# Closing the output blocks earlier: the last two experts by token block, block 0 with its last gathered row

## The chip, the core and the metric

The kernel runs on one core of a Trainium2 chip. The core has five engines, each with an instruction stream of its own that is executed in order: TensorE (PE, matrix products; its weight loads are shown as PEld), VectorE (DVE), ScalarE (ACT, with activation tables), GpSimd (POOL) and SyncE (SP, which here only issues DMA transfers). Engines wait for one another with semaphores. The metric is the device time of one execution in microseconds (us), smaller is better. The kernel before takes 2018.77 us (median of 3 runs, 2015.53 to 2018.92).

## The reference

One layer of a decoder trunk on 512 tokens of width 1024: three gated token mixers, and then a PEER channel mixer, in which each token picks 8 x 16 single-neuron experts out of 16384, and a final normalisation. What the change touches is the end:

```
x = x + peer_ffn(rms_norm(x, g_ffn), w_peer_q, peer_sub_keys, peer_u, peer_v)
return rms_norm(x, g_final)

def peer_ffn(h, w_q, sub_keys, u, v):              # per block of 128 tokens xb
    ...                                            # ids, gate: the 8 x 16 best experts of each token
    act = gelu(einsum('nd,nhkd->nhk', xb, u[ids]))
    wgt = gate * act
    return einsum('nhk,nhkd->nd', wgt, v[ids])

def rms_norm(x, g):
    return x * rsqrt(mean(x * x, axis=-1) + 1e-6) * g
```

## The kernel before

The 512 tokens lie in four blocks of 128 (`NB = 4`); the residual stream is the tile `x1`, 128 partitions by 4 blocks by 1024. Everything up to the PEER mixer takes the first 784 us, retrieval of the experts and the building of gate matrices the next 248 us. Then two kinds of work run side by side.

*Block 0* (`GB = 1`) is computed sparsely, by `gathered` (L1318 to L1336): GpSimd fetches the 128 rows of `u` and then the 128 rows of `v` that each token chose, one row per token and transfer (`ug`); DVE forms a dot product of each row of `u` with the token (L1328), and adds each weighted row of `v` to `x1[:, 0]` (L1334).

*Blocks 1 to 3* (`ND = 3`, 384 tokens) are computed densely, by `experts` (L1352 to L1384): all 16384 experts, in 128 tiles of 128, each masked by the gate matrix. Per tile of experts: a load of 128 rows of `v` (`vload`, 512 KB, tile `wr`), split by ACT and DVE into a high and a low part (`wh` at L127, `wl` at L128); the hidden values `hg` times the gate tile `gj` (`gh`, L1370); a split of that product (`wgh` at L127, `wgl` at L128); and 18 products of 512 columns on TensorE (L1383): three (high by high, low by high, high by low) for each of two halves of the width and three token blocks. They accumulate over all 128 tiles in six PSUM banks `acc_o`, named `S`, `S`, `tr`, `tr`, `o`, `o`: two halves each for blocks 1, 2 and 3. The loop runs one tile ahead: in step n it prepares tile n + 1 and then issues the products of tile n. The buffers `wr`, `wh`, `wl`, `gh`, `wgh` and `wgl` are double, so the `wh` of a tile waits until the products of two tiles before have been issued through.

In the text an "expert" is one such tile of 128. The hidden values of the first 32 (`LEAD`) are computed early, while the gate matrices are built, and written to DRAM (`hd`); these 32 come last in the loop's order, and in their steps TensorE has only the 18 products, and SyncE issues three kinds of load: `wr` (512 KB), `hg` (192 KB) and, every eighth step, `gj` (1536 KB).

The order of all instructions on all engines is that of the program, which is written by hand. `weave` takes turns between the two generators: `experts` with the weight 750 and `gathered` with 258, so `gathered` ends some 30 experts before the end. Pools of tiles (`sbuf`) are stacked; a pool opened where another was closed takes its place, and its first writer waits for the last reader of what lay there.

After both generators have ended, the tail closes the blocks in the order 0, 1, 2, 3 (L1437 to L1449): it loads the gain row `gl` as a broadcast to 128 partitions; adds the two accumulators of a block to `x1` (L1445; block 0 has none); squares the block on ACT with an accumulated sum (`rms_stats`, L166), takes the square root of the scaled sum (L168, with a table load ahead of the first one), the reciprocal on DVE (L170), multiplies block, reciprocal and gain on DVE (L1448) and writes 512 KB out (L1449).

Of the kernel before, what the change touches and what calls it, by code (L numbers as in the profile page):

```python
# [10 lines left out]
F32 = mybir.dt.float32  # L11
# [4 lines left out]
AF = mybir.ActivationFunctionType  # L16
OP = mybir.AluOpType
# [5 lines left out]
NB = 4  # L23
D = 1024
KD = 8
M = 256
EPS = 1e-6
# [9 lines left out]
def weave(*streams):  # L37

    live = [[0.0, w, iter(gen)] for gen, w in streams]
    while live:  # L40
        item = min(live, key=lambda x: x[0])
        try:
            c = next(item[2])
            item[0] += (c if c else 1.0) / item[1]
        except StopIteration:
            live.remove(item)


def drain(gen):
    for _ in gen:  # L50
        pass
# [53 lines left out]
def layer(ctx: ExitStack, tc: tile.TileContext, A: dict, out: bass.AP, dbg=None):  # L105
    nc = tc.nc
    v, s, g, pe = nc.vector, nc.scalar, nc.gpsimd, nc.tensor
# [6 lines left out]
    def sbuf(stack, name, side="left"):  # L114
        return stack.enter_context(tc.tile_pool(name=name, bufs=1, side=side, reuse_waits="tile"))

    def psum(tag, shape, bufs=2, dt=F32):
        return ps.tile(shape, dt, tag=tag, name=tag, bufs=bufs)
# [7 lines left out]
    def split(hi, lo, src, eng=None):  # L126
        s.activation(hi, src, AF.Copy)  # L127
        (eng or v).tensor_tensor(lo, src, f(hi), op=OP.subtract)  # L128
# [3 lines left out]
    def wload(src, nk, n, pool=None, eng=None):  # L132

        pool = pool or wpool
        raw = pool.tile([128, nk * n], F32, tag="wr", name="wr", bufs=2)
        nc.sync.dma_start(raw, src)
        hi = pool.tile([128, nk, n], F32R, tag="wh", name="wh", bufs=2)
        lo = pool.tile([128, nk, n], F32R, tag="wl", name="wl", bufs=2)
        split(hi, lo, raw.rearrange("p (k n) -> p k n", n=n), eng or g)
        return hi, lo  # L140
# [19 lines left out]
    def bcast_row(dst, src):  # L160
        nc.sync.dma_start(dst, bass.AP(tensor=src.tensor, offset=src.offset, ap=[[0, 128], [1, D]]))

    def rms_stats(pool, rows):
        sq = pool.tile([128, D], F32, tag="sq", name="sq")
        ss = pool.tile([128, 1], F32, tag="ss", name="ss", bufs=2)
        s.activation(sq, rows, AF.Square, accum_out=ss)  # L166
        rt = pool.tile([128, 1], F32, tag="rt", name="rt", bufs=2)
        s.activation(rt, ss, AF.Sqrt, bias=eps, scale=1.0 / D)  # L168
        rs = pool.tile([128, 1], F32, tag="rs", name="rs", bufs=2)
        v.reciprocal(rs, rt)  # L170
        return rs
# [15 lines left out]
    GB = 1  # L187
    ND = NB - GB
# [178 lines left out]
    V = [ap_.tile([128, NB, 4, 2, 64], F32R, name=f"V{br}") for br in range(2)]  # L367
# [189 lines left out]
    for c in cross_order:  # L557
        n = int(c[1]) if c[1:].isdigit() else None
# [18 lines left out]
        elif len(c) == 3:  # L577
            br, b = int(c[1]), int(c[2])
# [393 lines left out]
    for at in attention():  # L972
# [5 lines left out]
        while done < goal:  # L978
            c = next(filler, None)
# [27 lines left out]
    x1 = xp.tile([128, NB, D], F32, name="x1")  # L1007
# [95 lines left out]
    hst = ExitStack()  # L1103
# [29 lines left out]
    def q_scores(hp, qT):  # L1133
        sp = psum("o", [128, NB, 128])
        for b in range(NB):
            pe.matmul(sp[:, b], qT[:, b * 128:(b + 1) * 128], skt[:, hp], start=b == 0, stop=b == 3,
                      skip_group_check=True)
        ss = qp_.tile([128, NB, 128], F32, name="ssb", bufs=2)
        s.activation(ss, sp, AF.Copy)
        return ss  # L1140
# [38 lines left out]
    for hp in range(16):  # L1179
# [3 lines left out]
        ss = q_scores(hp, qT)  # L1183
# [72 lines left out]
    def hidden(w):  # L1256
        p = psum("z", [128, T])
        mm3(p[:, 0:NT], w, (hfh, hfl), KD, xs=lambda x, k: x[:, k, t0:T])
        hg = ep.tile([128, NT], F32, name="hg", bufs=4)
        s.activation(hg, p[:, 0:NT], AF.Gelu)  # L1260
        return hg
# [49 lines left out]
    def gather(src, b, k):  # L1311
        row = ex_[0].tile([128, D], F32, tag="ug", name="ug", bufs=8)
        g.indirect_dma_start(out=row, out_offset=None, in_=src,  # L1313
                             in_offset=bass.IndirectOffsetOnAxis(ap=ids[:, b, k:k + 1], axis=0))
        return row

    def gathered(b):
        act = ex_[0].tile([128, 128], F32, name="act")  # L1318
        wgt = ex_[0].tile([128, 128], F32, name="wgt")
        todo = [(A["u_rows"], k) for k in range(128)] + [(A["v_rows"], k) for k in range(128)]  # L1320
        rows = {}
        for n in range(256 + AHEAD):
            if n < 256:
                rows[n] = gather(todo[n][0], b, todo[n][1])
            m = n - AHEAD
            if 0 <= m < 128:
                jk = ex_[0].tile([128, D], F32, name="jk")
                v.scalar_tensor_tensor(jk, rows.pop(m), 1.0, hf[:, b], op0=OP.mult, op1=OP.mult,  # L1328
                                       accum_out=act[:, m:m + 1])
            if m == 127:  # L1330
                s.activation(wgt, act, AF.Gelu)
                v.tensor_tensor(wgt, wgt, gate[:, b], op=OP.mult)
            if m >= 128:
                v.scalar_tensor_tensor(x1[:, b], rows.pop(m), wgt[:, m - 128:m - 127], x1[:, b],  # L1334
                                       op0=OP.mult, op1=OP.add)
            yield 1  # L1336

    acc_o = []

    order = list(range(LEAD, 128)) + list(range(LEAD))  # L1340
    U, G, V, H = {}, {}, {}, {}

    def gload(q_):
        G[q_] = wv2.tile([128, NT // 16, 8, 16], F32, name="gj", bufs=2)
        nc.sync.dma_start(G[q_].rearrange("p g c t -> p g (c t)"), gd[order[8 * q_] // 8])

    def vload(m):
        j = order[m]
        V[m] = wload(A["v_rows"][j * 128:(j + 1) * 128], 2, 512, wv2, v)

    def experts():
        acc_o.extend(psum(("S", "S", "tr", "tr", "o", "o")[i], [128, 512]) for i in range(2 * ND))  # L1352
        for n in range(-1, 128):
            m = n + 1
            if m < 128:
                j = order[m]
                if j >= LEAD:
                    U[m] = feed.take(("u", j))
                if m:
                    vload(m)  # L1360
                if m % 8 == 4 and m + 4 < 128:
                    gload(m // 8 + 1)
                if j < LEAD:
                    H[m] = ep.tile([128, NT], F32, tag="hg", name="hg2", bufs=4)
                    nc.sync.dma_start(H[m], hd[j])
                yield 3.9
                if j >= LEAD:
                    H[m] = hidden(U.pop(m))
                gh = ep.tile([128, NT], F32, name="gh", bufs=2)
                v.tensor_tensor(gh.rearrange("p (g t) -> p g t", t=16), G[m // 8][:, :, m % 8],  # L1370
                                H.pop(m).rearrange("p (g t) -> p g t", t=16), op=OP.mult)
                wh = ep.tile([128, NT], F32R, name="wgh", bufs=2)
                wl = ep.tile([128, NT], F32R, name="wgl", bufs=2)
                split(wh, wl, gh)
                V[m] = (wh, wl, V[m])
                if j >= LEAD:
                    yield 3.9
            if n >= 0:
                wh, wl, vw = V.pop(n)
                for b in range(ND):  # L1380
                    for i, (a, c) in enumerate(((wh, vw[0]), (wl, vw[0]), (wh, vw[1]))):
                        for half in range(2):
                            pe.matmul(acc_o[2 * b + half], a[:, b * 128:(b + 1) * 128], c[:, half],  # L1383
                                      start=n == 0 and i == 0, stop=n == 127 and i == 2)  # L1384

    gst = ExitStack()
    gp = sbuf(gst, "gp", "right")
# [40 lines left out]
    rqs.close()  # L1428
    ex_.append(sbuf(hst, "ex", "right"))
    wv2 = sbuf(hst, "wv2", "right")  # L1430
    vload(0)
    gload(0)
    drain(ld)
    weave((experts(), 750), (gath, 258 * GB))
    hst.close()

    with ExitStack() as fst:  # L1437
        fin = sbuf(fst, "fin", "right")
        gl = fin.tile([128, D], F32, name="gl")
        bcast_row(gl, A["g_final"])  # L1440
        for b in range(NB):
            if b >= GB:
                for half in range(2):
                    xs = x1[:, b, half * 512:(half + 1) * 512]
                    v.tensor_tensor(xs, xs, acc_o[2 * (b - GB) + half], op=OP.add)  # L1445
            rs = rms_stats(fin, x1[:, b])
            ob = fin.tile([128, D], F32, name="ob", bufs=2)
            v.scalar_tensor_tensor(ob, x1[:, b], rs, gl, op0=OP.mult, op1=OP.mult)  # L1448
            nc.sync.dma_start(out[b * 128:(b + 1) * 128], ob)  # L1449


def _consts():
# [83 lines left out]
```

## Time and profile before

| | us |
|---|---|
| median of 3 runs | 2018.77 (2015.53 to 2018.92) |
| profiled execution | 2020.64 |
| its span, first to last instruction | 2018.9 |
| start of the span to the query stage | 784 |
| query stage, retrieval, gate matrices (784 to 1032) | 248 |
| TensorE at rest between the stages (1032.1 to 1054.7) | 22.6 |
| experts with hidden values computed, beside the gathered block (1054.7 to 1866) | 811 |
| experts with stored hidden values (1866 to 2003.6) | 138 |
| after the last product (2003.6 to 2018.9) | 15.3 |

Over the whole span TensorE is busy 94%, DVE 66%, ACT 42%, GpSimd 34% of the time. The last gathered row is added at 1874.8 to 1876.0. A row of the timeline has the start, the duration, engine, line, operation, the tile written and those read, the shape, and in brackets the idle time of the engine just before it and who ended it. SPq is SyncE's queue; its rows are the issue of a transfer and not the transfer itself. Busy times of DMA are a mean over the core's 16 DMA engines. A span of several matrix products (x2, x8) runs from the start of the first to the end of the last; products overlap by a part of their length.

### The profile page before, as it was taken

To read this page: it belongs to the slowest core of one execution; us is meant where nothing else is said; L and a number is where in the kernel's file an instruction comes from. 1 tells how busy PE (TensorE), PEld (TensorE's weight loads), DVE (VectorE), ACT (ScalarE), POOL (GpSimd) and SP (SyncE) were. 2 spreads that over 40 slices of the span, in tenths; PEclk is the share of its full clock that TensorE was granted. 3 is DMA by queue.
4 is the path that set the end of the run, shared out by engine and by line. 5 is a ranking of instruction groups with operands and counts; after the bars stand their busy time and mean duration, and the time that the engine had idled before them with its cause. 6 is when DMAs were issued, how large, how long until landed. Compare 5 with 4: busy or idle time off the path is not lost.

```text
span 2018.9 us, 27913 instructions
## 1 busy us (share of the span) xinstructions
PE 1904.6 (94%) x10155; PEld 1661.6 (82%) x10155; DVE 1340.6 (66%) x2722; ACT 856.7 (42%) x1427; POOL 690.7 (34%) x551
## 2 busy tenths in 40 slices
PE   8999999999999996888849999999999999999996
PEld 7888888888888786887749999889888889988785
DVE  4353167765532699788737778777777877878555
ACT  6433266666522332657643333333333333333333
POOL 3223555555443231000013444444444444543000
PEclk9999999999999998999879999999999999999998
DMA  5315621212134221458797888898888888888663
GB/s 191 101 61 167 203 76 52 69 48 64 59 99 147 84 84 44 142 160 254 224 302 285 315 298 320 301 317 304 321 323 306 306 323 319 311 305 305 220 206 138
DMA packets 161918, 411.58 MB, mean 204 GB/s; under 512 B 13890, under 2 KB 72002, under 8 KB 159092
## 3 DMA queue, kind: packets, MB, share of 16 engines
q1 hardware_dynamic: 124916, 275.56, 40.1%
q0 software_dynamic: 36864, 134.23, 19.1%
q8 instruction: 80, 1.31, 0.3%
q14 instruction: 58, 0.48, 0.1%
HBM read 376.15 MB, written 38.84 MB: 206 GB/s over the span
## 4 chain that ended last, share of the span: by engine, by line
PE 54%; DVE 22%; DMA 12%; issue 6%; ACT 5%; SPq 0%; POOL 0%; ACTq 0%; DVEq 0%
PE z L148 28%; DMA wr<-in_v_rows_dram 9%; PE S L1383 5%; PE tr L1383 5%; PE o L1383 5%; DVE wl L128 4%; DVE x L1334 3%; PE o L900 2%; PE S L857 2%; ACT wh L127 2%; DVE jk L1328 2%; PE tr L889 2%; DMA wr<-in_u_t_dram 1%; DVE ob L1288 1%; DVE eq L1285 1%
## 5 line engine op out<-in xcount | busy, mean ns | idle before, releaser
L127 ACT ACTIVATE wh<-wr 128x1024 fp32r<-128x1024 f32 (+2 forms) x364 | 373.3, 1028 | 383.2 <-DMA wr<-in_v_rows_dram 223.9
L128 DVE TENSOR_TENSOR wl<-wr,wh 128x1024 fp32r<-128x1024 f32 x260 | 314.7, 1222 | 244.5 <-ACT wh L127 234.0
L148 PE MATMUL z<-hfh,wh 128*128 128x384 f32 (+1 forms) x1144 | 398.6, 348 | 26.8 <-ACT wh L127 26.8
L148 PE MATMUL z<-hfl,wh 128*128 128x384 f32 (+1 forms) x1144 | 394.3, 345 | 0.0
L1313 POOL DMA_INDIRECT ug<-in_u_rows_dram,ids x128 | 178.6, 1395 | 503.8 <-ACT stg L1302 257.8
L128 POOL TENSOR_TENSOR wl<-wr,wh 128x1024 fp32r<-128x1024 f32 (+2 forms) x104 | 226.6, 2180 | 322.5 <-ACT wh L127 253.1
L1313 POOL DMA_INDIRECT ug<-in_v_rows_dram,ids x128 | 183.7, 1435 | 218.3 <-DVE x L1334 194.0
L148 PE MATMUL z<-hfh,wl 128*128 128x384 f32 (+1 forms) x1144 | 232.4, 345 | 25.8 <-DVE wl L128 25.8
L148 PEld LDWEIGHTS z<-hfh,wh 128*128 128x128 f32 x1144 | 219.4, 192 | 37.1 <-ACT wh L127 28.4
L148 PEld LDWEIGHTS z<-hfh,wl 128*128 128x128 f32 x1144 | 204.3, 190 | 32.9 <-DVE wl L128 28.1
L148 PEld LDWEIGHTS z<-hfl,wh 128*128 128x128 f32 x1144 | 219.2, 192 | 8.8
L127 ACT ACTIVATE wgh<-gh 128x384 fp32r<-128x384 f32 x128 | 67.2, 525 | 340.1 <-DVE gh L1370 336.4
L1334 DVE SCALAR_TENSOR_TENSOR x<-ug,wgt,x 128x1024 f32<-128x1024 f32 x128 | 163.9, 1280 | 1.2
L1328 DVE SCALAR_TENSOR_TENSOR jk<-ug,hf 128x1024 f32<-128x1024 f32 x128 | 156.1, 1220 | 1.1
L148 PE MATMUL z<-hnh,wh 128*128 128x512 f32 x384 | 152.2, 396 | 3.0 <-ACT wh L127 2.9
L148 PE MATMUL z<-hnl,wh 128*128 128x512 f32 x384 | 150.4, 392 | 0.0
L128 DVE TENSOR_TENSOR wgl<-gh,wgh 128x384 fp32r<-128x384 f32 x128 | 71.9, 561 | 78.3 <-ACT wgh L127 78.3
L878 POOL TENSOR_SCALAR pr<-pr,sm,gsig 128x128 f32<-128x128 f32 (+3 forms) x128 | 78.7, 619 | 88.1 <-DVE sm L936 55.8
L892 DVE TENSOR_TENSOR PB<-tr,PB 128x128 fp32r<-128x128 f32 (+3 forms) x128 | 62.5, 489 | 62.2 <-ACT PB L891 61.7
L148 PE MATMUL z<-hnh,wl 128*128 128x512 f32 x384 | 99.2, 393 | 0.0
L1260 ACT ACTIVATE hg<-z 128x384 f32<-128x384 f32 x128 | 61.4, 480 | 87.8 <-PE z L148 84.6
L148 PEld LDWEIGHTS z<-hnh,wh 128*128 128x128 f32 x384 | 72.1, 188 | 18.8 <-ACT wh L127 3.5
(346 smaller groups left out, 3554.6 us busy)
## 6 DMA issues: line engine op xcount, KB each, us to landing
wr<-in_u_t_dram SPq DMA_DIRECT2D x128, 512.0 KB
wr<-in_v_rows_dram SPq DMA_DIRECT2D x128, 512.0 KB
wr<-in_w_z_dram SPq DMA_DIRECT2D x48, 512.0 KB
gd<-stg SPq DMA_DIRECT2D x24, 1024.0 KB
gj<-gd SPq DMA_DIRECT2D x16, 1536.0 KB
wr<-in_w_peer_q_dram SPq DMA_DIRECT2D x16, 512.0 KB
hd<-hg SPq DMA_DIRECT2D x32, 192.0 KB
hg<-hd SPq DMA_DIRECT2D x32, 192.0 KB
```

The costliest lines, as they stand in the source:

```text
L127: s.activation(hi, src, AF.Copy)
L128: (eng or v).tensor_tensor(lo, src, f(hi), op=OP.subtract)
L148: pe.matmul(p, w[a][:, k], xs(x[b], k), start=k == 0 and a == 0 and b == 0, stop=k == nk - 1 and a == 1)
L857: pe.matmul(sp[:, 0:nn], Q[gq, r][:, qb * 128:(qb + 1) * 128], KK[gq, br][i][:, 0:nn], start=i == 0, stop=i == 1)
L878: g.tensor_scalar(pr[:, 0:n], pr[:, 0:n], sm, gsig[:, qb, c:c + 1], op0=OP.mult, op1=OP.mult)
L889: pe.transpose(pt[:, kb], pr[:, kb * 128:(kb + 1) * 128], ident)
L892: return lambda: v.tensor_tensor(lo, pt[:, 0:qb + 1], f(hi), op=OP.subtract)
L1260: s.activation(hg, p[:, 0:NT], AF.Gelu)
L1313: g.indirect_dma_start(out=row, out_offset=None, in_=src, in_offset=bass.IndirectOffsetOnAxis(ap=ids[:, b, k:k + 1], axis=0))
L1328: v.scalar_tensor_tensor(jk, rows.pop(m), 1.0, hf[:, b], op0=OP.mult, op1=OP.mult, accum_out=act[:, m:m + 1])
L1334: v.scalar_tensor_tensor(x1[:, b], rows.pop(m), wgt[:, m - 128:m - 127], x1[:, b], op0=OP.mult, op1=OP.add)
L1383: pe.matmul(acc_o[2 * b + half], a[:, b * 128:(b + 1) * 128], c[:, half], start=n == 0 and i == 0, stop=n == 127 and i == 2)
```

## The change

Three things, in `gathered`, in `experts` and in what stood behind them.

- `closing(b)` is new. It does what the tail did for a block, but in two halves of 512 columns: addition of the accumulator (blocks 1 to 3), square with accumulated sum on ACT; the first half's sum is scaled by 1/1024 and given the epsilon on DVE, and it serves as the bias of the square root that has the second half's sum as input. `finish(b)` takes the root, the reciprocal and writes the block out as two halves of 256 KB. `closing` of one block calls `finish` of the one before it.
- In `experts` the step for expert 126 issues no products. The step for 127 issues those of 126 and 127 together, by token block: block 1's for both, `closing(1)`, block 2's for both, `closing(2)`, block 3's for both, `closing(3)`.
- `gathered` ends with `closing(0)` and `finish(0)`. The pool `fin` is opened, and `gl` is loaded, ahead of the first `vload`; `finish(3)` comes last.

In the order of instructions: on SyncE `gl` now stands between the last two writes of gate matrices (`gd`) and the first `wr` of `v`; block 0's two output transfers stand between the `hg` load of one expert and the `wr`, `gj` and `hg` loads of the next. On ACT block 0's two squares, a table load and the root stand between a `wh` and the next `wgh`; on DVE the scaling, the reciprocal and the two output multiplications stand between a `wl` and the next `gh`. GpSimd's order is the same. The number of products is the same; those of experts 126 and 127 have another order.

```diff
@@ gathered @@
                 v.scalar_tensor_tensor(x1[:, b], rows.pop(m), wgt[:, m - 128:m - 127], x1[:, b],
                                        op0=OP.mult, op1=OP.add)
             yield 1
+        closing(b)
+        finish(last.pop())
+
+    last, FS = [], {}
+
+    def finish(b):
+        rt = fin.tile([128, 1], F32, tag="rt", name="rt", bufs=4)
+        s.activation(rt, FS.pop((b, 1)), AF.Sqrt, bias=FS.pop((b, 0)), scale=1.0 / D)
+        rs = fin.tile([128, 1], F32, tag="rs", name="rs", bufs=4)
+        v.reciprocal(rs, rt)
+        for half in range(2):
+            c = slice(half * 512, half * 512 + 512)
+            ob = fin.tile([128, 512], F32, tag="fob", name="fob", bufs=4)
+            v.scalar_tensor_tensor(ob, x1[:, b, c], rs, gl[:, c], op0=OP.mult, op1=OP.mult)
+            nc.sync.dma_start(out[b * 128:(b + 1) * 128, c], ob)
+
+    def closing(b):
+        for half in range(2):
+            xs = x1[:, b, half * 512:half * 512 + 512]
+            if b >= GB:
+                v.tensor_tensor(xs, xs, acc_o[2 * (b - GB) + half], op=OP.add)
+            sq = fin.tile([128, 512], F32, tag="fsq", name="fsq")
+            ss = FS[b, half] = fin.tile([128, 1], F32, tag=f"fs{half}", name="fs", bufs=4)
+            s.activation(sq, xs, AF.Square, accum_out=ss)
+            if half == 0:
+                v.tensor_scalar(ss, ss, 1.0 / D, EPS, op0=OP.mult, op1=OP.add)
+        for d in last:
+            finish(d)
+        last[:] = [b]
@@ experts @@
-            if n >= 0:
-                wh, wl, vw = V.pop(n)
-                for b in range(ND):
+            if n < 0 or n == 126:
+                continue
+            for b in range(ND):
+                for k in ((126, 127) if n == 127 else (n,)):
+                    wh, wl, vw = V[k]
                     for i, (a, c) in enumerate(((wh, vw[0]), (wl, vw[0]), (wh, vw[1]))):
                         for half in range(2):
                             pe.matmul(acc_o[2 * b + half], a[:, b * 128:(b + 1) * 128], c[:, half],
-                                      start=n == 0 and i == 0, stop=n == 127 and i == 2)
+                                      start=k == 0 and i == 0, stop=k == 127 and i == 2)
+                if n == 127:
+                    closing(GB + b)
+            V.pop(n)
@@ the end of layer @@
     wv2 = sbuf(hst, "wv2", "right")
+    fin = sbuf(hst, "fin", "right")
+    gl = fin.tile([128, D], F32, name="gl")
+    bcast_row(gl, A["g_final"])
     vload(0)
     gload(0)
     drain(ld)
     weave((experts(), 750), (gath, 258 * GB))
+    for b in last:
+        finish(b)
     hst.close()
-
-    with ExitStack() as fst:
-        fin = sbuf(fst, "fin", "right")
-        gl = fin.tile([128, D], F32, name="gl")
-        bcast_row(gl, A["g_final"])
-        for b in range(NB):
-            if b >= GB:
-                for half in range(2):
-                    xs = x1[:, b, half * 512:(half + 1) * 512]
-                    v.tensor_tensor(xs, xs, acc_o[2 * (b - GB) + half], op=OP.add)
-            rs = rms_stats(fin, x1[:, b])
-            ob = fin.tile([128, D], F32, name="ob", bufs=2)
-            v.scalar_tensor_tensor(ob, x1[:, b], rs, gl, op0=OP.mult, op1=OP.mult)
-            nc.sync.dma_start(out[b * 128:(b + 1) * 128], ob)
```

## The prediction

> **What bounds it.** I read the page's slices first (TensorE close to full in nearly all of them), then busy time by stretch, then the timeline of the three places that the diff touches: the closing of block 0 near 1875 us, the last two experts, and everything after the last product.
>
> ```profile
> 1878.00:2003.60 125.60, 125.59 (x538) 100.55 (x537) 68.08 (x91) 47.62 (x62) 0.00 (x0) 1.00 0.58 199
> 2003.60:2018.90 15.30, 0.00 (x0) 0.00 (x0) 6.73 (x10) 4.33 (x9) 0.00 (x0) 0.64 0.32 127
> ```
>
> Columns: stretch, length, busy us (instructions) of PE, weight load, DVE, ACT, POOL, then granted clock, DMA share, GB/s. From 1878 on TensorE never rests: 125.6 / 538 = 0.233 us per 512-wide product, 18 x 0.233 = 4.2 us per expert. A TensorE stall put into this stretch is therefore paid in full. The 15.3 us after the last product have no TensorE work at all; only there can the change gain.
>
> **The tail it wants to shorten.** Before, block 3 ends so:
>
> ```profile
> 2010.75 1.28 DVE L1445 TENSOR_TENSOR x<-x,o 128x512 f32<-128x512 f32 x2
> 2012.07 1.06 ACT L166 ACTIVATE sq<-x 128x1024 f32<-128x1024 f32 x1 [2.75 <-DVE x L1445]
> 2013.03 0.19 ACT L166 ACTIVATION_READ_ACCUMULATOR sq<-x 128x1 f32 x1
> 2013.25 0.29 ACT L168 ACTIVATE rt<-ss,eps 128x1 f32<-128x1 f32 x1
> 2013.57 0.16 DVE L170 RECIPROCAL rs<-rt 128x1 f32<-128x1 f32 x1 [1.54 <-ACT rt L168]
> 2013.77 1.28 DVE L1448 SCALAR_TENSOR_TENSOR ob<-x,rs,gl 128x1024 f32<-128x1024 f32 x1
> ```
> ```profile
> 2015.50:2017.40 1.90, 0.00 (x0) 0.00 (x0) 0.00 (x0) 0.00 (x0) 0.00 (x0) 0.50 0.69 276
> ```
>
> Each block is a chain of 4.2 us and three of them follow one another, with block 0's in front. The last `ob` ends at 2015.05; issue, transfer (the second fence: 276 GB/s x 1.9 us, the 512 KB of the last output) and receipt take the other 3.85 us to 2018.9.
>
> **Part 1: products by block, blocks in halves (tail).** No product is added; what moves is that the S products of expert 127 come 6 instead of 18 products after those of 126 begin. Its operands do not come earlier, because ACT, DVE and the loads keep their order:
>
> ```profile
> 1994.80 1.06 ACT L127 ACTIVATE wh<-wr 128x1024 fp32r<-128x1024 f32 x1 [0.77 <-PE o L1383]
> 1997.70 0.53 ACT L127 ACTIVATE wgh<-gh 128x384 fp32r<-128x384 f32 x1 [1.84 <-DVE gh L1370]
> 1998.26 0.56 DVE L128 TENSOR_TENSOR wgl<-gh,wgh 128x384 fp32r<-128x384 f32 x1 [0.67 <-ACT wgh L127]
> ```
> ```profile
> 1995.03 0.63 PE L1383 MATMUL S<-wh,wgh 128*128 128x512 f32 x2
> ...
> 2002.96 0.63 PE L1383 MATMUL o<-wl,wgh 128*128 128x512 f32 x2
> ```
>
> `wh` of 127 waits for the buffer that 125's products release (1994.80), then `wl`, `gh`, `wgh` follow; `wgh` is done at 1998.23. Expert 126 starts at 1995.03; its six S products end at 1996.43. So TensorE waits 1.8 us for `wgh`, and about 0.2 more for `wgl` (1998.82) and restarts: products end 2.0 us later. In before's clock: S complete 2000.0, tr 2002.8, o 2005.6.
>
> The closings then run: per half an addition (1.28 / 2 = 0.64), a square of 512 with its accumulator read; the first half's sum is scaled by a small DVE instruction *before* DVE may add the second half.
>
> ```profile
> L1041 ACT ACTIVATE sq<-x 128x512 f32<-128x512 f32 x8 | 5.0, 630 | 11.1 <-DVE x L1038 9.3 <-ACT sq L1041 1.8
> 1999.29 1.28 ACT L168 ACT_TABLE_LOAD   x1
> ```
>
> With 0.63 + 0.19 less 0.09 overlap = 0.73 for a square: block 2's first addition starts at 2002.7 (when tr is done), square to 2004.1, scale to 2004.3, second half added to 2004.9, squared to 2005.65, root of block 1 to 2006.0, reciprocal to 2006.2, block 1's two outputs to 2007.45. Only now does DVE take block 3's first addition, though its products ended at 2005.6: DVE and ACT are the bound again. Block 3: added 2008.1, squared 2008.85, scaled 2009.0, added 2009.65, squared 2010.4; block 2's root, reciprocal and two outputs to 2012.2 stand ahead of block 3's reciprocal (2012.3); its outputs end at 2012.95 and 2013.6. That is 1.45 us before 2015.05. The last transfer is half as large: the 3.85 us become about 3.3 (an estimate from the 1.9 us of data: half of it, 0.95, would be saved if the other half were through by then; it is issued only 0.65 earlier, so about 0.55 is). Tail together: 2.0 us gained; bounds: 3.0 if the wait for `wgh` were free, 0.5 if the closings interlock worse. The table load (1.28 us) leaves the tail but lay beside TensorE's last products.
>
> **Part 2: block 0 closed with its last gathered row.** These instructions leave a place where they ran beside expert 127 and enter every queue near 1876 us:
>
> ```profile
> 1874.76 1.28 DVE L1334 SCALAR_TENSOR_TENSOR x<-ug,wgt,x 128x1024 f32<-128x1024 f32 x1
> 1875.96 0.55 DVE L1370 TENSOR_TENSOR gh<-gj,hg 128x384 f32<-128x384 f32 x1
> 1877.18 0.56 DVE L128 TENSOR_TENSOR wgl<-gh,wgh 128x384 fp32r<-128x384 f32 x1 [0.67 <-ACT wgh L127]
> 1878.13 1.23 DVE L128 TENSOR_TENSOR wl<-wr,wh 128x1024 fp32r<-128x1024 f32 x1 [0.39 <-ACT wh L127]
> 1879.28 0.55 DVE L1370 TENSOR_TENSOR gh<-gj,hg 128x384 f32<-128x384 f32 x1
> ```
> ```profile
> 1877.06 1.04 ACT L127 ACTIVATE wh<-wr 128x1024 fp32r<-128x1024 f32 x1
> 1879.94 0.53 ACT L127 ACTIVATE wgh<-gh 128x384 fp32r<-128x384 f32 x1 [1.84 <-DVE gh L1370]
> ```
> ```profile
> 1881.62 0.63 PE L1383 MATMUL S<-wh,wgh 128*128 128x512 f32 x2
> ...
> 1885.83 0.63 PE L1383 MATMUL S<-wh,wgh 128*128 128x512 f32 x2
> ```
>
> Call the experts whose products start at 1881.62 and 1885.83 B and C. The new order puts the closing between B's `wl` (1878.13) and B's `gh` (1879.28) on DVE, and between `wh` (1877.06) and `wgh` (1879.94) on ACT. ACT: two squares from 1878.1 to 1879.55, table load to 1880.9, root to 1881.2. DVE has the scale, then waits, reciprocal to 1881.4, two outputs to 1882.7; only then B's `gh`, 3.4 us late. B's `wgh` is ready at 1883.85, when TensorE wanted it at 1881.62: a stall of 2.3 us, 2.5 with the restart. Those who wait on this: B's products, and through them all later ones.
>
> The larger price is SyncE's queue:
>
> ```profile
> 1874.87 0.33 SPq L136 DMA_DIRECT2D wr<-in_v_rows_dram  x1
> 1875.25 0.42 SPq L1345 DMA_DIRECT2D gj<-gd  x1
> 1875.73 0.43 SPq L1365 DMA_DIRECT2D hg<-hd  x1
> 1879.39 0.33 SPq L136 DMA_DIRECT2D wr<-in_v_rows_dram  x1
> ```
> ```profile
> 1875.50:1882.00 6.50, 6.50 (x28) 4.86 (x27) 3.82 (x6) 2.59 (x4) 0.00 (x0) 1.00 0.94 355
> ```
>
> SyncE issues C's three loads at 1874.87 to 1875.73. In the changed order block 0's two output issues stand ahead of them, and they wait for the outputs at 1882.1 and 1882.7. So `wr` of C goes out at about 1883.15, 8.3 us late, `gj` at 1883.55, `hg` at 1884.0. Window row: 355 GB/s x 6.5 us = 2.3 MB, which is `wr`, `gj` and `hg` (0.52 + 1.57 + 0.20 MB); the small `hg` has landed only when that much is through, at 1882.0, 7.1 us after the issue of `wr`. Moved: 1883.15 + 7.1 = 1890.25. C's `gh` needs that `hg`: 1890.3; `wgh` 0.66 behind its start and 0.53 long: ready 1891.5; products of C at 1891.55 instead of 1885.83. Together with a slower restart this is 5.9 us, the 2.5 us of B contained in it. D's `wr`, issued at 1884.6 and next in the line, lands near 1892.1 (0.5 MB more): split, `gh`, `wgh` done by 1895.6, before C's products end at 1896.0; no more is lost. Bounds: 2.5 (the loads hidden after all) and 7.8 (the 512 KB written ahead of `wr` add their own 1.9 us). I take 5.9, since `wr`, `gj` and `hg` are the same transfers as in the row.
>
> **Clock.** B leaves a TensorE gap of 2.3 us, C one from the end of B's products (1883.9 + 4.4 = 1888.3) to 1891.55, above 3 us. Before shows what gaps do:
>
> ```profile
> 842.05 1.69 PE L148 MATMUL z<-hfh,wl 128*128 128x384 f32 x8 [2.34 <-DVE wl L128]
> 853.55 2.50 PE L148 MATMUL z<-hfh,wl 128*128 128x384 f32 x8 [1.91 <-DVE wl L128]
> 853.60:858.00 4.40, 4.40 (x17) 4.30 (x18) 4.30 (x8) 1.91 (x2) 0.00 (x0) 0.61 0.56 164
> ```
>
> After a gap of 2.34 us eight products took 1.69 us, after one of 1.91 us 2.50: the granted clock there was 0.61 over 4.4 us, that is 0.39 x 4.4 = 1.7 us of full clock lost. A gap above 3 us I expect to cost this once: 1.5 us (bounds 0 and 3, the tail's 1.8 us gap included). [...]
>
> **Part 3: `gl` and the new pool.** The 512 KB broadcast moves from 1989.65 to ahead of the first load of V.
>
> ```profile
> 1028.48 3.92 SPq L1304 DMA_DIRECT2D gd<-stg  x2
> 1048.88 0.35 SPq L136 DMA_DIRECT2D wr<-in_v_rows_dram  x1
> ...
> 1054.71 0.69 PE L148 MATMUL z<-hfh,wh 128*128 128x384 f32 x1 [22.62 <-ACT wh L127]
> 1048.50:1050.00 1.50, 0.00 (x0) 0.00 (x0) 0.00 (x0) 0.00 (x0) 0.00 (x0) 0.50 0.12 8
> ```
>
> TensorE stands still there until that load is split. `gl` is issued right behind the gate writes, at about 1032.5; its data follow theirs and fall mostly into the 1.5 us in which the queue moves 8 GB/s. Bounds 0 and 3 us; I take 0.5.
>
> **Sum.** -2.0 + 5.9 + 1.5 + 0.5 = +5.9 us. The profiled execution took 2020.64 (span 2018.9), 1.9 above the median; on the median 2018.77 that is 2024.7.
>
> **Rivals.**
> - *Covered closing* (not slower): ACT and DVE idle enough that block 0's closing hides and C's loads still arrive. It needs C's `hg` landed by 1883.6, so SyncE's issue by about 1876.5, but the outputs it waits for are made after 1881. Then only the tail counts: 2018.77 - 2.0 = 2016.8. Chance 0.08.
> - *Only DVE pays*: the late loads are quick, since nothing else is in the queue, and catch up with B's delay: -2.0 + 2.5 + 0.5 = +1.0, 2019.8. Against it: `gj` of 1.5 MB between `wr` and `hg`. Chance 0.18.
> - *No half clock*: 2023.2. For it the 2.34 us row, against it the 1.91 us row. Chance 0.17. [...]
> - *Heavier*: the tail's gap halves the clock too and `gl` delays the first load by 2 us or more: +1.5 +1.7 = 2027.9. Chance 0.15.
> - The forecast: 0.42, own range 2022.5 to 2027.
>
> **Chances.** 0.2% is 4 us, about what a measurement of this kernel can tell from no change: bounds 2014.7 and 2022.8. Faster takes half of the first rival and a little for what I do not see, 0.05; within takes the rest of the first, the second and the lower part of the third and of the forecast, 0.32; slower the remaining 0.63. The range 2018 to 2029 leaves out the first rival and the end of the heavier one.
>
> **What would show it.** In the profile after: DVE's `gh` of the expert behind block 0's outputs about 3.4 us late; the next `wr` issue behind the output issues; TensorE gaps of about 2.3 and 3.3 us near 1882 to 1892 and one of 1.8 us before the S products of 127, granted clock below 1 behind one; from the last product to the end 11 to 12 us instead of 15.3; no table load there. I am wrong if TensorE has no gap behind block 0's closing, or if the last products' end moves by less than 4 us.

## The result, and the profile after

The changed kernel takes 2024.55 us (median of 15 runs, 2017.72 to 2028.54), the kernel before 2018.92 us in the same comparison (15 runs, 2014.00 to 2022.40). The ratio is 1.0027, with a 95% interval of 1.0017 to 1.0036: slower by 3.4 to 7.3 us. The profiled execution took 2028.54 us (span 2026.8), 7.9 us more than that of before (span 2018.9). The steps below are accounted in these two executions; 2.3 us of their difference do not stand in the medians: the profiled execution is the slowest of its 15.

The closing of block 0 on DVE, from the timeline of the kernel after (start, duration, operation, tiles, shape, and the idle time before it with its ender):

```profile
1878.57 1.22 DVE L128 TENSOR_TENSOR wl<-wr,wh 128x1024 fp32r<-128x1024 f32 x1 [0.39 <-ACT wh L127]
...
1881.56 0.16 DVE L1347 RECIPROCAL rs<-rt 128x1 f32<-128x1 f32 x1 [1.70 <-ACT rt L1345]
1881.76 1.41 DVE L1351 SCALAR_TENSOR_TENSOR fob<-x,rs,gl 128x512 f32<-128x512 f32 x2
1883.09 0.55 DVE L1400 TENSOR_TENSOR gh<-gj,hg 128x384 f32<-128x384 f32 x1
...
1892.62 0.56 DVE L1400 TENSOR_TENSOR gh<-gj,hg 128x384 f32<-128x384 f32 x1 [1.88 <-DMA hg<-hd]
```

The same place on ACT, which DVE waited 1.70 us for, and in SyncE's queue of issues:

```profile
1879.94 1.28 ACT L1345 ACT_TABLE_LOAD   x1
...
1888.43 1.06 ACT L127 ACTIVATE wh<-wr 128x1024 fp32r<-128x1024 f32 x1 [4.18 <-DMA wr<-in_v_rows_dram]
```
```profile
1882.54 1.00 SPq L1352 DMA_DIRECT2D out_dram<-fob  x2
1883.63 0.39 SPq L136 DMA_DIRECT2D wr<-in_v_rows_dram  x1
1884.08 0.44 SPq L1375 DMA_DIRECT2D gj<-gd  x1
1884.57 0.42 SPq L1395 DMA_DIRECT2D hg<-hd  x1
1885.10 0.36 SPq L136 DMA_DIRECT2D wr<-in_v_rows_dram  x1
```

In the order of the prediction's letters: B's `gh` follows block 0's outputs at once, at 1883.09. C's three loads are issued only after both output issues, from 1883.63 on, and C's `gh` starts at 1892.62 with the landing of `hg`; the last issue shown is D's `wr`. The 1.5 MB of `gj` are not for C: the program loads them for the eight experts from number 104 on, and C is number 100, but C's `hg` stands behind them in the queue. What TensorE makes of it (same view, TensorE's rows; the first is the start behind the rest between the stages):

```profile
1054.73 0.69 PE L148 MATMUL z<-hfh,wh 128*128 128x384 f32 x1 [22.85 <-ACT wh L127]
...
1884.31 0.77 PE L1415 MATMUL S<-wh,wgh 128*128 128x512 f32 x2 [2.08 <-ACT wgh L127]
...
1893.85 0.73 PE L1415 MATMUL S<-wh,wgh 128*128 128x512 f32 x2 [3.44 <-ACT wgh L127]
...
1899.81 0.63 PE L1415 MATMUL S<-wh,wgh 128*128 128x512 f32 x2
...
2004.81 0.63 PE L1415 MATMUL S<-wh,wgh 128*128 128x512 f32 x2
...
2008.07 0.74 PE L1415 MATMUL S<-wh,wgh 128*128 128x512 f32 x2 [1.70 <-ACT wgh L127]
```

The others are the first S products of B, C, D (the expert after C), 126 and 127. Before, B started at 1881.62, C at 1885.83 and D at 1890.03. The rests of 2.08 and 3.44 us are new, and so is the 1.70 before the S products of 127. Busy time by stretch (columns as in the prediction: stretch, length, PE, PEld, DVE, ACT, POOL, granted clock, DMA share, GB/s):

```profile
1884.50:1892.60 8.10, 5.91 (x18) 4.20 (x17) 1.57 (x2) 1.06 (x1) 0.00 (x0) 0.79 1.01 358
1885.30:1892.60 7.30, 5.11 (x16) 3.69 (x15) 1.22 (x1) 1.06 (x1) 0.00 (x0) 0.80 0.99 372
1884.87:1888.28 3.41, 3.41 (x9) 2.71 (x9) 0.00 (x0) 0.00 (x0) 0.00 (x0) 0.50 0.98 302
1895.10:1898.50 3.40, 3.40 (x10) 2.62 (x9) 2.20 (x3) 0.52 (x1) 0.00 (x0) 0.50 0.44 119
2015.46:2026.80 11.34, 0.00 (x0) 0.00 (x0) 5.99 (x12) 2.11 (x9) 0.00 (x0) 0.61 0.38 139
```

While C's loads are under way the DMA engines are full (shares of 1.01 and 0.99, first two rows; the second begins where both of block 0's outputs have landed). Behind each of the two rests TensorE runs 3.4 us at half clock (granted clock 0.50, third and fourth row). After the last product 11.3 us are left instead of 15.3 (last row).

The 7.9 us, from these rows against those of before:

| step | us | how |
|---|---|---|
| ahead of the closing | +0.44 | the expert before B starts at 1877.64 and not 1877.20 |
| B late | +2.25 | 1884.31 - 1881.62 - 0.44 |
| C late, beyond B | +5.33 | 1893.85 - 1885.83 = 8.02, less 2.69 |
| C's products, half clock and restart | +1.76 | C to D takes 5.96 and not 4.20 |
| rest before 127's S products | +2.1 | last product ends 11.87 later, 9.78 of it from above |
| after the last product | -4.0 | 11.34 and not 15.30 |

### The profile page after: what moved, and what is told of

It is laid out like the page before. It is cut to its first block, busy times and chain, and to the rows that moved or that the text cites. A ratio compares the mean times of both kernels' runs of the same rounds, so it can differ in the third digit from the quotient of the medians.

```text
span 2026.8 us, 27937 instructions
## 1 busy us (share of the span) xinstructions
PE 1908.5 (94%) x10155; PEld 1662.9 (82%) x10155; DVE 1342.3 (66%) x2730; ACT 858.3 (42%) x1435; POOL 688.4 (34%) x551
## 4 chain that ended last, share of the span: by engine, by line
PE 62%; DVE 19%; DMA 9%; ACT 5%; issue 4%; SPq 0%; POOL 0%; ACTq 0%; DVEq 0%
PE z L148 32%; PE tr L1415 7%; PE S L1415 6%; PE o L1415 6%; DMA wr<-in_v_rows_dram 6%; DVE wl L128 3%; DVE x L1334 3%; PE o L900 2%; PE S L857 2%; ACT wh L127 2%; PE tr L889 2%; DMA wr<-in_u_t_dram 1%; DVE ob L1288 1%; DVE eq L1285 1%; DVE oa L1283 1%
## 5 line engine op out<-in xcount | busy, mean ns | idle before, releaser
L1415 PE MATMUL S<-wh,wgh 128*128 128x512 f32 x256 | 81.5, 400 | 12.0 <-ACT wgh L127 11.9
```

## The experiments

Single executions of one kernel scatter by 8 to 16 us from lowest to highest, those of before too, and most of that arises before the places that the change touches (the last product of hidden values starts between 1852 and 1861 us). So for each run the stretch from the start of that last product to the end of the span is given beside the ratio. It is read from TensorE's rows in the timeline of the profiled execution. Each ratio is to executions of the kernel before that were taken beside that run:

| kernel | to 126's first S product | from there to the end | sum | ratio to before, 95% interval |
|---|---|---|---|---|
| before | 137.66 | 23.84 | 161.5 | |
| after | 147.78 | 21.96 | 169.7 | 1.0027 (1.0017 to 1.0036) |
| block 0 late | 137.63 | 24.33 | 162.0 | 1.0002 (0.9986 to 1.0019) |
| block 0 early alone | 146.15 | 22.06 | 168.2 | 1.0044 (1.0029 to 1.0059) |
| old product order | 146.77 | 22.14 | 168.9 | 1.0051 (1.0036 to 1.0065) |
| outputs behind loads | 142.12 | 23.48 | 165.6 | 1.0017 (1.0003 to 1.0031) |
| outputs one step later | 141.85 | 21.95 | 163.8 | 1.0009 (0.9995 to 1.0022) |
| gaps filled | 145.47 | 21.96 | 167.4 | 1.0024 (1.0013 to 1.0036) |
| block 0 in pieces | 137.78 | 21.94 | 159.7 | 0.9993 (0.9979 to 1.0007) |
| pieces and plain tail | 137.00 | 17.56 | 154.6 | 0.9967 (0.9951 to 0.9983) |

The stretch scatters too. The change, "block 0 early alone" and "old product order" run the same instructions up to expert 126 and take 147.78, 146.15 and 146.77 us, so a difference of 1.6 us between single executions shows nothing there; the four kernels without a rest behind block 0 (before, block 0 late and the two in pieces) lie between 137.00 and 137.78.

The theory: the change loses in one place, behind block 0's closing, through DVE and ACT (B), SyncE's queue (C) and the clock; and it gains 2 us in the tail through halves and product order. Rivals: the product order or the early `gl` costs the time; the queue matters little and DVE alone pays; the clock plays no part; the tail's gain has another source.

**Each part alone.** Without the early closing of block 0, which goes ahead of block 1's in the last step:

```diff
@@ gathered @@
-        closing(b)
-        finish(last.pop())
@@ experts @@
+            if n == 127:
+                closing(0)
+                finish(last.pop())
             for b in range(ND):
```

> Products of 126 and 127 by block and closings in halves as in the change, but block 0 is closed in its old place, behind the last operand of expert 127. Theory (the loss lies in the closing of block 0 between the experts): no TensorE gap and no half clock near 1880 us, products end about 2 us later than before because of the wait for wgh of 127, and the tail is little shorter since block 0's outputs again stand ahead of DVE's first addition: 2019 to 2020 us against 2018.9 of before. Rival (the new order of the products is the loss): 2022 us or more.

The ratio is 1.0002 (0.9986 to 1.0019), and the way to expert 126 is that of before, 137.6 us. So the loss sits in block 0's early closing. The early `gl` and the new pool, which this kernel has too, show no cost: the rest between the stages, where they would be paid, lasts 22.73 us and 22.62 before (the ratio alone would leave room for 3.8 us). But the tail, with products by block and all halves, is not shorter: 24.3 us. DVE's rows:

```profile
2002.75 1.42 DVE L1349 SCALAR_TENSOR_TENSOR fob<-x,rs,gl 128x512 f32<-128x512 f32 x2
2004.08 0.68 DVE L1356 TENSOR_TENSOR x<-x,S 128x512 f32<-128x512 f32 x1
```

Block 1's first addition starts without idle time behind block 0's outputs, 7.75 us after 126's first S product at 1996.33. TensorE is slowed here from 2000.76 to 2004.17 (two products take 1.05 us and not 0.63, as behind C's rest in the change, where the granted clock is 0.50), behind its rest of 1.70 us ahead of 127's S products, but none of DVE's additions in this tail waits for a product, so that does not lengthen it. The other half, block 0 early with the old tail for blocks 1 to 3 (and two buffers for `fob` instead of four):

```diff
@@ experts @@
-            if n < 0 or n == 126:
+            if n < 0:
...
-                for k in ((126, 127) if n == 127 else (n,)):
+                for k in (n,):
...
-                if n == 127:
-                    closing(GB + b)
@@ the end of layer @@
-    for b in last:
-        finish(b)
+    fin2 = sbuf(hst, "fin2", "right")
+    for b in range(GB, NB):
...
+        rs = rms_stats(fin2, x1[:, b])
+        ob = fin2.tile([128, D], F32, name="ob", bufs=2)
```

> Only block 0 is closed early, with gl ahead of the first load of V; experts and the tail of blocks 1 to 3 are as before. Theory: both TensorE gaps (2.1 and 3.4 us) and one stretch at half clock that costs, 9 us together; the tail gains 1.7 us, for which DVE's first addition waited on block 0: about 2026 us. Rival (the early closing costs nothing, the loss is in the tail): 2017 us.

It loses like the change, 1.0044 (1.0029 to 1.0059), and its tail takes 22.06 us, 0.1 from that of the change. DVE's row of the first addition:

```profile
2004.42 1.29 DVE L1475 TENSOR_TENSOR x<-x,S 128x512 f32<-128x512 f32 x2 [1.76 <-PE S L1415]
```

It now waits for the products (126's first S product is at 1998.86, 5.56 us before) and no longer for block 0. So the tail's gain comes from block 0 having left it. And with the halves kept, only the product order put back:

```diff
-            if n < 0 or n == 126:
+            if n < 0:
...
-                for k in ((126, 127) if n == 127 else (n,)):
+                for k in (n,):
```

> As the change, but experts 126 and 127 issue their products one after the other as before; each block is closed in halves behind its last product. Theory (behind the last products DVE and ACT set the end, so TensorE's wait for wgh of 127 is mostly hidden): no gap of 1.7 us, products end 2 us earlier, the end only 0.4 us earlier: 2024.2 us. Rival (the products set the end): 2 us earlier, 2022.5 us.

Its tail takes 22.14 us, 0.2 more than the change, where 0.4 less was expected; the product order is worth no more than that. The ratio, 1.0051 (1.0036 to 1.0065), meets that of the change only at its lower end, but the two were taken beside different executions of before, and no difference between them is read from it. The way to 126 lost its time in other portions here: C follows B after 8.97 us, and C to D takes 6.96, at a granted clock of 0.58 (1886.98 to 1893.94). Where the pieces of the tail go, from DVE's rows of five kernels:

| kernel | 126's first S product to first addition | to the last output made | to the end |
|---|---|---|---|
| before | 7.28 | 12.74 | 3.81 |
| after | 4.85 | 14.10 | 3.00 |
| block 0 late | 7.75 | 13.59 | 2.99 |
| old product order | 5.57 | 13.59 | 2.98 |
| block 0 early alone | 5.56 | 12.76 | 3.74 |

Products by block let DVE begin 0.72 us earlier (4.85, 5.57), but the chain from there is 0.51 longer. The halves write the last output earlier (3.0 instead of 3.7) and pay 0.83 for it in a longer chain (13.59, 12.76). The rows of the kernel after show why:

```profile
2017.32 0.68 DVE L1358 TENSOR_TENSOR x<-x,o 128x512 f32<-128x512 f32 x1
2018.85 0.15 DVE L1363 TENSOR_SCALAR fs<-fs 128x1 f32<-128x1 f32 x1 [0.85 <-ACT fsq L1361]
2018.92 0.68 DVE L1358 TENSOR_TENSOR x<-x,o 128x512 f32<-128x512 f32 x1
2020.63 0.17 DVE L1347 RECIPROCAL rs<-rt 128x1 f32<-128x1 f32 x1 [1.03 <-ACT rt L1345]
2020.83 1.42 DVE L1351 SCALAR_TENSOR_TENSOR fob<-x,rs,gl 128x512 f32<-128x512 f32 x2
```

Between the two halves DVE waits 0.85 us for ACT's square, because the scaling of the first sum stands ahead of the second addition, and then 1.03 for the root. Only then do block 2's outputs come, and block 3's behind them.

**The queue.** Block 0's output issues are held back until `wr`, `gj` and `hg` of the following steps have been issued: until expert 127's loads, or only until the next step's.

```diff
@@ finish @@
-            nc.sync.dma_start(out[b * 128:(b + 1) * 128, c], ob)
+            held.append(lambda b=b, c=c, ob=ob: nc.sync.dma_start(out[b * 128:(b + 1) * 128, c], ob))
+            if b:
+                held.pop()()
@@ experts, behind the load of hg @@
+                if m == 127:
+                    while held:
+                        held.pop(0)()
```

> As the change, but SyncE issues the two output transfers of block 0 behind the last load instead of between two experts' loads. Theory (SyncE's queue is the larger part of the loss): the gap of 2.1 us before the products of the first expert behind the closing stays, the gap of 3.4 us before the second is gone, at most one stretch at half clock: 2019 to 2021.5 us. Rival (the work on ACT and DVE is the loss and the loads only follow): both gaps stay, 2024 us or more.

The second kernel has the same without the line `if m == 127`:

> As the change, but the two output transfers of block 0 stand behind wr, gj and hg of the second expert instead of ahead of them. Theory (what hurts is that these loads wait behind the outputs): the second gap of 3.4 us goes, or shrinks below 1 us, the third expert's wr is issued 3.5 us late and costs at most 1 us; from the last hidden product to the end 164 to 166 us, as with the outputs behind the last load (165.6), against 169.7 of the change and 161.5 of before. Rival (the writing of 512 KB beside the loads is the cost, wherever it is issued): the second gap stays above 2 us.

TensorE's rows of the first (to 127's loads), B and C:

```profile
1888.17 1.22 PE L1420 MATMUL S<-wh,wgh 128*128 128x512 f32 x2 [2.08 <-ACT wgh L127]
...
1893.96 0.63 PE L1420 MATMUL S<-wh,wgh 128*128 128x512 f32 x2
```

and of the second:

```profile
1883.30 0.73 PE L1419 MATMUL S<-wh,wgh 128*128 128x512 f32 x2 [2.09 <-ACT wgh L127]
...
1889.27 0.63 PE L1419 MATMUL S<-wh,wgh 128*128 128x512 f32 x2
```

B's rest stays at 2.08, C's is gone. The way to expert 126 shrinks by 5.7 and 5.9 us (147.78 to 142.12 and 141.85), and the ratios fall to 1.0017 and 1.0009. What is left over before in the second, +2.3 us in the sum, is B's 2.25 and the half clock, which now falls on B (5.97 from B to C and not 4.20, granted clock 0.50 from 1884.70 to 1888.10), less the tail's 1.9. In the first, 1.5 us came back in the tail: 23.48 instead of 21.95, with this stretch in it, also behind a rest of 1.7 us before 127's products. DVE waits 1.32 us for S and 1.85 for tr there, and 1.06 and 0.57 in the change. With B's (1888.10 to 1891.50, granted clock 0.50) that makes two half-clock stretches, where at most one was expected:

```profile
2007.50:2010.90 3.40, 3.40 (x10) 2.68 (x9) 1.44 (x3) 1.03 (x3) 0.00 (x0) 0.50 0.00 0
```

**The clock.** The rests are filled with products into a PSUM bank that nobody reads, 9 ahead of B's and 20 ahead of C's; the output isn't touched by them.

```diff
@@ gathered, behind finish(last.pop()) @@
+        warm.extend((0, 9, 20))
@@ experts, ahead of the products @@
+            if warm:
+                pz = psum("z", [128, 512])
+                cnt = warm.pop(0)
+                for i in range(cnt):
+                    pe.matmul(pz, hfh[:, 0, 0:128], hfh[:, 1], start=i == 0, stop=i == cnt - 1)
```

> As the change, with 9 products on resident data (into a bank that nobody reads) ahead of the products of the first expert behind block 0's closing, and 20 ahead of the second's: TensorE works through both gaps. Theory (the idle gaps halve the granted clock, and on the second expert that costs 1.7 us): full clock from 1875 us to the last operand of 127, the third expert starts 4.2 to 4.3 us behind the second instead of 5.96; the stretch from the last hidden product to the end is 168.0 us instead of 169.7. Rival (the products behind a gap are slow for another reason): the 5.96 us stay.

```profile
1882.27 0.73 PE L1421 MATMUL S<-wh,wgh 128*128 128x512 f32 x2
...
1886.70 4.73 PE L1415 MATMUL z<-hfh 128*128 128x512 f32 x20
1891.27 0.73 PE L1421 MATMUL S<-wh,wgh 128*128 128x512 f32 x2
...
1895.70 0.63 PE L1421 MATMUL S<-wh,wgh 128*128 128x512 f32 x2
```

In this view (TensorE's timeline) no rest is left, the granted clock is 1.00 from 1876 to 1896, and C to D takes 4.43 us instead of 5.96: the half clock cost 1.5 us, and the 0.23 left over 4.20 is the restart, in which TensorE's weight load waits 0.29 us for `wgl`. B to C still takes 9.00, so that wait is not the clock's. The interval of the ratio, 1.0024 (1.0013 to 1.0036), is too wide to show 1.5 us; the trace shows it.

**The closing without its price.** If B's and C's waits are the whole loss, then the same closing costs nothing when its instructions go where DVE and ACT are idle. Five pieces (first square; second square and scaling; root; reciprocal and first output; second output) go one by one behind the split of a step, or, for the root, between `wh` and `gh`; outputs are issued behind 127's loads:

```diff
@@ gathered @@
-        closing(b)
-        finish(last.pop())
+        parts.extend((("E", lambda: square(b, 0)), ("E", lambda: (square(b, 1), scale(b))), ("M", lambda: root(b)),
+                      ("E", lambda: (recip(b), write(b, 0))), ("E", lambda: write(b, 1))))
...
+    def piece_at(slot):
+        if parts and parts[0][0] == slot:
+            parts.pop(0)[1]()
@@ experts @@
+                piece_at("M")
                 gh = ep.tile([128, NT], F32, name="gh", bufs=2)
...
             V.pop(n)
+            piece_at("E")
```

> As the change, but block 0 is closed in five pieces spread over the experts behind its last row: the two squares and the scaling behind the products of two of them, the table load and the root between wh and wgh of a third (ACT idles 1.84 us there), the two output multiplications where DVE idles 1.28 us; the outputs are issued behind the last load. Theory (the closing hurts because it stands in one lump in all queues): all steps 4.2 to 4.3 us, no gap; from the last hidden product to the end 159.6 us, 1.9 less than before: 2017 us. Rival (any work put into this stage shows, since the chain wh, wl, gh, wgh, wgl has 0.4 us of slack per expert): 2 to 4 us more, no gain on before.

DVE's rows around the first output, and TensorE through the whole of these experts by stretch:

```profile
1886.58 0.15 DVE L1387 RECIPROCAL rs<-rt 128x1 f32<-128x1 f32 x1
1886.77 0.75 DVE L1392 SCALAR_TENSOR_TENSOR fob<-x,rs,gl 128x512 f32<-128x512 f32 x1
1887.96 1.22 DVE L128 TENSOR_TENSOR wl<-wr,wh 128x1024 fp32r<-128x1024 f32 x1 [0.44 <-ACT wh L127]
```
```profile
1870.00:2000.00 130.00, 128.30 (x547) 102.04 (x547) 72.41 (x100) 51.31 (x70) 0.00 (x0) 1.00 0.57 196
```

`wl` behind the output still waits 0.44 us for ACT, so the output cost nothing, and the granted clock is 1.00 all through. The way to 126 is 137.8 us as before, the tail 21.9 as in the change: 159.7 in the sum, 1.8 below before. The ratio, 0.9993 (0.9979 to 1.0007), doesn't tell it from before.

Last, the same with the product order of before and a tail in which both halves are added before a sum is scaled, and the previous block's outputs stand behind the next block's additions:

```diff
@@ the end of layer @@
-    for b in last:
-        finish(b)
+    for b in range(GB, NB):
+        for half in range(2):
+            add(b, half)
+            square(b, half)
+        if b == 2:
+            recip(1)
+            write(1, 0)
+            write(1, 1)
+        scale(b)
+        root(b)
+    for b in (2, 3):
+        recip(b)
+        write(b, 0)
+        write(b, 1)
```

> Block 0 in pieces as in the run before this; experts 126 and 127 issue their products one after the other as before; behind them DVE adds both halves of a block ahead of the scaling instruction, and the outputs of block 1 stand between block 2's and block 3's additions, those of blocks 2 and 3 last. Theory (behind the products DVE and ACT set the end, and in the change DVE waits there for ACT): products end at the time of before, the rest takes 9 to 10 us instead of 15.3; from the last hidden product to the end 155 to 156 us, 6 less than before: 2013 us. Rival (the tail is bound by transfer and receipt): 2 us less than before, 2017 us.

```profile
1999.60 1.28 DVE L1349 TENSOR_TENSOR x<-x,S 128x512 f32<-128x512 f32 x2 [1.77 <-PE S L1427]
2001.08 0.15 DVE L1357 TENSOR_SCALAR fs<-fs 128x1 f32<-128x1 f32 x1 [0.19 <-ACT fsq L1354]
2001.15 1.27 DVE L1349 TENSOR_TENSOR x<-x,tr 128x512 f32<-128x512 f32 x2
2002.35 0.16 DVE L1366 RECIPROCAL rs<-rt 128x1 f32<-128x1 f32 x1
2002.54 1.42 DVE L1371 SCALAR_TENSOR_TENSOR fob<-x,rs,gl 128x512 f32<-128x512 f32 x2
2003.87 0.15 DVE L1357 TENSOR_SCALAR fs<-fs 128x1 f32<-128x1 f32 x1
2003.93 1.28 DVE L1349 TENSOR_TENSOR x<-x,o 128x512 f32<-128x512 f32 x2
2005.40 0.15 DVE L1357 TENSOR_SCALAR fs<-fs 128x1 f32<-128x1 f32 x1 [0.19 <-ACT fsq L1354]
...
2007.18 1.42 DVE L1371 SCALAR_TENSOR_TENSOR fob<-x,rs,gl 128x512 f32<-128x512 f32 x2
```

From the first addition at 1999.60 to the last output at 2008.60 DVE is idle for two times 0.19 us (the second behind block 3's additions). That chain takes 9.0 us instead of 14.1, the tail from 126 on 17.56 instead of 21.96. The kernel takes 2012.58 us (9 runs; before takes 2017.81 beside it, 32 runs), a ratio of 0.9967 (0.9951 to 0.9983): it beats before, and with it the change.

## Why the prediction was right

It forecast 2024.7 us from the kernel before's 2018.77, +5.9; the medians differ by 5.6, the profiled executions by 7.9. Step by step:

- *B's stall, 2.5 us*: 2.25 measured, through the chain that was named. DVE waits 1.70 for the root, the outputs take 1.4, `gh` starts at 1883.09; by the forecast it was 1882.7 in before's clock, 1883.1 with the 0.44 of this execution.
- *C's late loads, 5.9 us with B's part in it*: the mis-sized term, 7.6 measured. The issue time was right (1883.63; forecast 1883.15 + 0.44), but the data of `hg` arrived 9.0 us behind it (1892.62) and not 7.1. The forecast took the same transfers as before and set aside its own upper bound, 7.8, in which the 512 KB of outputs issued just ahead take 1.9 us first. From 1884.50 to 1892.60 alone, 358 GB/s moved 2.9 MB, more than the 2.29 of `wr`, `gj` and `hg`. The outputs had landed by 1885.30 (2.5 and 2.1 us behind their issue), and from there to 1892.60 still 372 GB/s x 7.30 us = 2.72 MB were moved. So at least 0.43 MB of loads that were issued behind `hg` went through ahead of its end: D's, whose `wr` was issued 0.53 us behind `hg` (before, 3.66), and perhaps those of the expert after D, whose `wr` was issued at 1890.77. That is 1.2 us of the 1.9 by this estimate; how the rest divides between them and the outputs isn't settled. The forecast had D's `wr` "next in the line" behind `hg`. Its 7.1 us was also no landing that a row shows, but the length of a busy window; C's `gh` did not wait for `hg` before. In the other three kernels with this closing and this queue `hg` came 8.4 to 9.0 us behind the issue of `wr`, too, and C 9.0 to 9.5 us behind B (9.54 here). Whether `hg` issued ahead of `gj` would have come in time was not run. That the wait in SyncE's queue is the cause is shown by the two kernels that hold the output issues back.
- *Clock, 1.5 us once*: 1.76 in the trace with the restart, 1.5 by filling the rests. It varies with the execution: with the old product order C to D took 6.96 us, 2.8 over 4.20. Two rests led to a half-clock stretch (granted clock 0.50), but B's was free: its products ended at 1890.4, 3.4 us before C's operands came.
- *`gl`, 0.5 us*: at most 0.2. The rest between the stages lasts 22.85 us and not 22.62, and TensorE starts behind it at 1054.73, where it was 1054.71. In the other eight kernels, all with the early `gl`, it lasts 20.9 to 23.1 us, so no cost of `gl` is shown.
- *Tail, -2.0 us*: -1.9, with its two parts nearly as forecast (the last product 2.1 us later by the wait for `wgh`, 11.3 us behind it where 11 to 12 were forecast). But the forecast put this gain under part 1, and that attribution fell. Products by block and halves without block 0's departure gain nothing (24.33 against 23.84), and block 0's departure alone gives 22.06. The gain belongs to part 2, whose price stands near 1882. (The forecast's 1.8 us for the wait for `wgh` took 1996.43 as the end of 126's S products; that is the start of the next ones, the six end at 1996.59, and the wait was 1.70.)

So the total fitted closer than its terms, and that was luck: loads 1.7 us too low and clock 0.3 too low, `gl` 0.3 or more too high, and 0.4 of drift, against medians that differ by 2.3 us less than the profiled executions do. Which step was shorter in the other executions of the change isn't settled; the three kernels with the same closing show that both the loads and the clock vary by half a us and more.

The rivals each stood for a condition, and each was made: a covered closing (in pieces) gives 159.7 us of stretch, 1.8 below before where 2.0 was worked out; DVE alone paying (outputs a step later) +2.3 where it was +1.0 without a half clock; no half clock (rests filled) -2.3 against the change, 1.5 of it from C to D, where it was -1.5. In the change itself none of the three held. The heavier case did not come either: the tail's rest of 1.70 us brought no half clock in the change (granted clock 1.00 from 2008.07 to 2015.46), though behind the same rest TensorE was slowed with block 0 late (two products in 1.05 us) and with the outputs behind 127's loads (granted clock 0.50).

## What to carry to other kernels

Before moving a short chain to where its data are ready, list what each in-order queue holds behind it: here the closing of one block on two engines cost 2.3 us, and two output issues ahead of three loads another 5 to 6. Cut such a chain into pieces that go where each engine is idle anyway, and issue outputs behind the loads. In a closing tail read the idle times of the one engine that binds it: splitting into halves gained nothing while each half waited for the other engine, and putting both additions first, with the previous block's outputs behind them, took 4.4 us off (21.94 to 17.56; the product order of before came back with it).

## What the runs showed of the hardware

What TensorE did behind a rest, by the granted clock or, where no clock was read, by the time of two products of 512 columns in its rows:

| kernel | rest, us | behind it |
|---|---|---|
| before, 853.55 | 1.91 | 0.61 from 853.60 to 858.00 |
| before, 842.05 | 2.34 | 1.00 from 842.10 to 850.00 |
| before, 1866.86 and 1872.69 | 0.64 and 1.24 | 1.00 from 1866 to 1878 |
| after, B | 2.08 | 0.50 from 1884.87 to 1888.28 |
| after, C | 3.44 | 0.50 from 1895.10 to 1898.50 |
| after, 127 | 1.70 | 1.00 from 2008.07 to 2015.46 |
| block 0 late, 127 | 1.70 | two products in 1.05 us from 2000.76 to 2004.17 |
| block 0 in pieces, 127 | 1.70 | 1.00 from 1870 to 2000 |
| block 0 early alone, B | 2.07 | two products in 0.63 us from 1879.70 on |
| block 0 early alone, C | 4.93 | two products in 1.22 and 1.05 us from 1888.06 to 1890.79 |
| old product order, B | 2.09 | two products in 1.05 us from 1879.96 to 1882.52 |
| old product order, C | 2.85 | 0.58 from 1886.98 to 1893.94 |
| outputs behind loads, B | 2.08 | 0.50 from 1888.10 to 1891.50 |
| outputs behind loads, 127 | 1.70 | 0.50 from 2007.50 to 2010.90 |
| outputs one step later, B | 2.09 | 0.50 from 1884.70 to 1888.10 |
| gaps filled, B and C | none | 1.00 from 1876 to 1896 |

So in the cases of this table TensorE was slowed behind a rest of 1.70 us in two of four, behind one of 1.91 us, behind 2.07 to 2.09 us in four of five, and behind 2.85, 3.44 and 4.93 us; behind 2.34 us in the kernel before the clock stayed at 1.00. The length of the rest alone does not tell the cases apart; what does was not shown. With the rests filled C to D takes 4.43 us, and 5.96 in the change.
